# Moving the first stage's weight loads to GpSimd's queue, and packing the round trip of the inverse, in a hybrid HGRN2 and RWKV-7 layer

## The chip, the core and the metric

The kernel runs on one NeuronCore of a Trainium2 chip. The metric is device time in microseconds (us) of one execution, less being better. The kernel before takes 2757.54 us, the median of three runs (2757.54 to 2757.74).

## What is computed

One decoder layer over 2048 tokens of width 1024, in float32. Two token mixers work side by side on the columns of one input projection, then follows a ConvFFN.

```python
h = _rmsnorm(x, norm1_w[l])
proj = h @ w_in[l]                                   # 1024 -> 3840 columns
o_hg = _hgrn2_mixer(...)                             # 4 heads of 128, gated linear recurrence, chunks of 64
rw_p = rw_p + (_token_shift(rw_p) - rw_p) * rw_shift_mu[l]
o_rw = _rwkv7_mixer(...)                             # 8 heads of 64, S_t = S diag(w) + (S a) b^T + v k^T
x = x + jnp.concatenate([o_hg, o_rw], axis=-1) @ w_out[l]
x = x + _conv_ffn(_rmsnorm(x, norm2_w[l]), w_up[l], conv_w[l], conv_b[l], w_down[l])
return _rmsnorm(x, final_norm_w)
```

The kernel computes the RWKV-7 recurrence chunk by chunk. In each chunk of 64 tokens a unit triangular matrix must be inverted; its two 32x32 diagonal blocks are inverted by elimination, and the rest by small products.

## The kernel before

**Two stages.** The first stage (`phase1`, up to about 1385 us of the span) does the input projection, both mixers and the output projection of three of the four token blocks of 512. The second stage does the ConvFFN. The diff touches the first stage alone.

**The dense stream.** Products with the big weights are made in float32r from a high and a low part of each operand, three matmuls each (`mm3`, L259 to L261, into `pj`). The projection has 30 columns of 128 for each of 4 token blocks. In the first block each half column is loaded from `w_in` (256 KB, `wraw`, L550), split into `wh` and `wl` by ScalarE (L243) and VectorE (L244), and both parts are stored to a DRAM tile `Win` from GpSimd's queue (L553). In the other three blocks `wh` and `wl` are loaded back from `Win` (L557). `out_block` loads `w_out` in 32 pieces of 256 KB (`woraw`, L382) for each of three token blocks and splits them in the same way. `wh` and `wl` have 4 buffers each. `wraw` is a ring of 4 buffers that `woraw`, `oraw`, `xh` and other tiles share. All loads of weights, of tokens and of intermediate results are issued from SyncE's queue (SP), in order.

**The RWKV stream** (`rw_super`) runs 8 times, each for two pairs of heads and 512 tokens. `u` is the pair, `e` the chunk within a pair of chunks, `b` the pair of chunks, `h` the head of the pair. Its steps, by the line of their matmuls:
- L705 with L708: the products that fill `M`.
- L721: 8 DMAs copy the 32x32 diagonal blocks of `M` to DRAM (`Ed`), matrix by matrix. L723 loads them back as `E`, one matrix on each of 64 partitions.
- L729 to L755: transposes and products that need no inverse.
- L774 and L776: VectorE inverts the 64 blocks in 31 steps, into `Ti`.
- L780 and L782: `Ti` and its transpose go to DRAM (`Td`). L789 and L792 bring them back by 12 DMAs, 8 into `TTs` and 4 into `TZ`.
- L800 (`z`), L813 (`z2`) and L826 (`qus`): products with the inverse.
- ScalarE copies `qus` (PSUM) into `M` and `UV`: for `u` = 0 the part for `M` and then two for `UV`; for `u` = 1 the copies for `M` and `UV` alternate.
- L851 (`yg`), L867 and L874 (`xp`, `yp`), and L885 with L887, a chain over 8 chunks in which each product waits for VectorE's `XH` of the chunk before.

PSUM tiles of this stream come from `bank2()`, with two buffers in all, so a new tile waits until every reader of the tile before the last is done.

**The HGRN stream** (`hg_unit`) runs 16 times, with products at L965 to L1033; its VectorE steps share that engine's order with the inverse.

**Order.** The three streams are Python generators, drawn in turn; a framework's scheduler then lays the instructions out on each engine by its own costs, and each engine runs them in that order. The last token block's results (`oT`, L918 and L1039) are stored from GpSimd's queue, those of the others from SP's.

## Time and profile before

| | |
|---|---|
| Median of three runs | 2757.54 us |
| Profiled execution | 2750.25 us |
| Its span, first to last instruction | 2748.5 us |
| Mean granted clock of TensorE | 0.982 |
| TensorE matmul (PE) busy | 2645.1 us (96%) |
| VectorE (DVE) busy | 1964.0 us (71%) |
| ScalarE (ACT) busy | 1329.2 us (48%) |
| GpSimd (POOL) busy | 75.7 us (3%) |
| SP's DMA queue (q1) | 476.49 MB, 53.9% of 16 engines' span |
| GpSimd's DMA queue (q0) | 34.11 MB, 3.4% |

The profile comes from one execution, so a sum of its parts is compared with 2750.25 us, and a difference is then taken from the median of 2757.54 us. Busy matmuls are pipelined and their ends are modelled, so 96% doesn't say that TensorE runs at its peak; what matters is where it stands idle, for what it waits there, and at which clock it runs.

### The profile page before, as it was taken

What the parts mean: (1) busy time and instruction counts of PE and PEld (TensorE: products, weight loads), DVE (VectorE), ACT (ScalarE), POOL (GpSimd) and SP (SyncE); (2) the same over time, 40 slices, a digit from 0 to 9 for tenths busy, and PEclk for the clock granted to TensorE, in tenths of its full rate; (3) what the DMA queues carried; (4) which work ended last, traced back from release to release, by engine and by line L of the source; (5) the groups of instructions that cost most, each with busy time, mean ns of one, the idle gap of its engine ahead of it and who ended that gap; (6) DMA issues with size and microseconds to landing.
All of it is one profiled execution on the core that took longest, in us unless ns stands there. A gap on an engine that the chain in (4) does not pass through costs nothing.

```text
span 2748.5 us, 47939 instructions
## 1 busy us (share of the span) xinstructions
PE 2645.1 (96%) x18059; PEld 2108.0 (77%) x18059; DVE 1964.0 (71%) x3697; ACT 1329.2 (48%) x2124; POOL 75.7 (3%) x144
## 2 busy tenths in 40 slices
PE   8999999989999899999989999998999999999998
PEld 6777777767777667778668788886888888777887
DVE  5868666585576765757567789988997787667656
ACT  5455342544534444343346754555545455445544
POOL 3211000000000000000000000000000000000000
PEclk9999999989999999999999999999999999999999
DMA  9555544345653456743584467746662224999865
GB/s 302 197 163 169 166 133 127 118 133 183 209 168 120 140 158 216 239 167 121 152 279 145 126 206 260 243 143 225 220 221 75 91 86 157 312 329 311 287 195 184
DMA packets 396029, 513.68 MB, mean 187 GB/s; under 512 B 73503, under 2 KB 200853, under 8 KB 395797
## 3 DMA queue, kind: packets, MB, share of 16 engines
q1 hardware_dynamic: 385137, 476.49, 53.9%
q0 software_dynamic: 10592, 34.11, 3.4%
q8 instruction: 142, 2.33, 0.4%
q14 instruction: 90, 0.74, 0.1%
q10 hardware_dynamic: 68, 0.02, 0.0%
HBM read 373.12 MB, written 137.36 MB: 186 GB/s over the span
## 4 chain that ended last, share of the span: by engine, by line
PE 60%; DVE 7%; DMA 5%; ACT 2%; issue 2%; SPq 1%; DVEq 0%; ACTq 0%
PE ua L261 5%; PE ua L259 5%; PE ua L260 5%; PE pj L259 5%; PE pj L260 4%; PE pj L261 4%; PE ud L259 3%; PE ud L260 3%; PE ud L261 3%; PE da L260 2%; PE da L261 2%; PE da L259 2%; PE db L260 2%; PE db L259 2%; PE db L261 2%
## 5 line engine op out<-in xcount | busy, mean ns | idle before, releaser
L259 PE MATMUL pj<-hh,wh 128*128 128x512 f32 x960 | 401.8, 419 | 0.8 <-DVE xh L398 0.6
L261 PE MATMUL pj<-hh,wl 128*128 128x512 f32 x960 | 379.7, 396 | 0.4 <-DMA wl<-Win191l 0.4
L260 PE MATMUL pj<-hl,wh 128*128 128x512 f32 x960 | 379.7, 396 | 0.0
L259 PE MATMUL ua<-Bh,uwh 128*128 128x512 f32 x704 | 278.7, 396 | 14.9 <-ACT uwh L243 14.1
L261 PE MATMUL ua<-Bh,uwl 128*128 128x512 f32 x704 | 276.3, 393 | 0.3 <-DVE uwl L244 0.3
L260 PE MATMUL ua<-Bl,uwh 128*128 128x512 f32 x704 | 276.1, 392 | 0.0
L259 PEld LDWEIGHTS pj<-hh,wh 128*128 128x128 f32 x960 | 181.3, 189 | 53.4 <-issue 12.4
L260 PEld LDWEIGHTS pj<-hl,wh 128*128 128x128 f32 x960 | 181.4, 189 | 40.3 <-issue 6.0
L261 PEld LDWEIGHTS pj<-hh,wl 128*128 128x128 f32 x960 | 180.9, 188 | 39.6 <-issue 0.7
L243 ACT CAST uwh<-uraw 128x512 fp32r<-128x512 f32 x220 | 134.5, 618 | 140.9 <-PE ua L260 71.4
L243 ACT CAST dah<-draw 128x512 fp32r<-128x512 f32 x151 | 93.8, 621 | 184.6 <-PE da L260 50.5
L244 DVE TENSOR_TENSOR uwl<-uraw,uwh 128x512 fp32r<-128x512 f32 x220 | 147.3, 688 | 46.9 <-ACT uwh L243 46.8
L244 DVE TENSOR_TENSOR dal<-draw,dah 128x512 fp32r<-128x512 f32 x151 | 104.3, 690 | 104.9 <-ACT dah L243 104.6
L259 PEld LDWEIGHTS ua<-Bh,uwh 128*128 128x128 f32 x704 | 133.4, 190 | 43.7 <-ACT uwh L243 14.7
L261 PEld LDWEIGHTS ua<-Bh,uwl 128*128 128x128 f32 x704 | 133.3, 189 | 30.1 <-DVE uwl L244 2.2
L260 PEld LDWEIGHTS ua<-Bl,uwh 128*128 128x128 f32 x704 | 133.7, 190 | 27.2
L259 PE MATMUL ud<-Bh,uwh 128*128 128x512 f32 x352 | 137.8, 392 | 1.9 <-DVE cv L1357 1.9
L261 PE MATMUL ud<-Bh,uwl 128*128 128x512 f32 x352 | 137.1, 389 | 0.0
L260 PE MATMUL ud<-Bl,uwh 128*128 128x512 f32 x352 | 137.0, 389 | 0.0
L260 PE MATMUL da<-dbl,dah 128*128 128x512 f32 x340 | 134.2, 395 | 0.7 <-DVE dbl L244 0.2
L261 PE MATMUL da<-dbh,dal 128*128 128x512 f32 x340 | 133.2, 392 | 0.0
L259 PE MATMUL da<-dbh,dah 128*128 128x512 f32 x340 | 128.3, 391 | 1.6 <-ACT dbh L243 1.5
(434 smaller groups left out, 5792.2 us busy)
## 6 DMA issues: line engine op xcount, KB each, us to landing
uraw<-in_w_up_dram SPq DMA_DIRECT2D x176, 256.0 KB, 3.2
woraw<-in_w_out_dram SPq DMA_DIRECT2D x96, 256.0 KB, 3.5
draw<-Sg SPq DMA_DIRECT2D x88, 256.0 KB, 3.5
draw<-Tw SPq DMA_DIRECT2D x88, 256.0 KB, 3.7
gd<-y SPq DMA_DIRECT2D x86, 256.0 KB, 2.9
xt<-x1d SPq DMA_DIRECT2D x32, 512.0 KB, 5.3
draw<-gd SPq DMA_DIRECT2D x63, 256.0 KB, 5.0
draw<-in_w_down_dram SPq DMA_DIRECT2D x63, 256.0 KB, 5.2
```

The costliest lines, as they stand in the source:

```text
L243: S.copy(hi, src)
L244: V.tensor_sub(lo, src, hi.bitcast(F32))
L259: TE.matmul(acc, lh, rh, start=first, stop=False, skip_group_check=skip)
L260: TE.matmul(acc, lh, rl, start=False, stop=False, skip_group_check=skip)
L261: TE.matmul(acc, ll, rh, start=False, stop=last, skip_group_check=skip)
```

## The change

Three edits, all in the first stage:
- `wload` stands for GpSimd's queue, and the loads of `wraw`, of `Win` (360 of them) and of `woraw` are issued from it instead of from SP's. The 120 stores to `Win` and the last block's `oT` stores were on that queue already.
- `M` is laid out with `e` ahead of `u`, and `Ed` and `Td` have the two pairs of a block next to each other, so that one DMA serves both pairs: 4 transfers into `Ed` instead of 8, and 6 out of `Td` instead of 12. With the load of `E` and the two stores to `Td` that makes 13 for each of the 8 runs instead of 23. The bytes are the same.
- After `qus`, ScalarE makes the three copies into `M` first, for both pairs, and then the four into `UV`.

```diff
+        wload = nc.gpsimd.dma_start
...
-                        dma(raw, w_out[0, k * P:(k + 1) * P, dh * 512:dh * 512 + 512])
+                        wload(raw, w_out[0, k * P:(k + 1) * P, dh * 512:dh * 512 + 512])
...
-                            dma(raw, w_in[0, k2 * 512:k2 * 512 + 512, cols[i]:cols[i] + P].rearrange("(k p) c -> p k c", p=P))
+                            wload(raw, w_in[0, k2 * 512:k2 * 512 + 512, cols[i]:cols[i] + P].rearrange("(k p) c -> p k c", p=P))
...
-                                dma(ws[k2][c].bitcast(F32), Win[ct][k2][c])
+                                wload(ws[k2][c].bitcast(F32), Win[ct][k2][c])
...
-            for u in U:
-                for e in range(2):
-                    for q in range(2):
-                        r0 = er0(e) + 32 * q
-                        m0 = u * 32 + (e * 2 + q) * 8
-                        dma(Ed[m0:m0 + 8].rearrange("m s t -> s m t"),
-                            M[r0:r0 + 32, u, e, :, :, 32 * q:32 * q + 32].rearrange("p b h t -> p (b h) t"))
+            for e in range(2):
+                for q in range(2):
+                    r0 = er0(e) + 32 * q
+                    m0 = (e * 2 + q) * 16
+                    dma(Ed[m0:m0 + 16].rearrange("m s t -> s m t"),
+                        M[r0:r0 + 32, e, :, :, :, 32 * q:32 * q + 32].rearrange("p u b h t -> p (u b h) t"))
...
-            for u in U:
-                for e in range(2):
-                    r0 = er0(e)
-                    for q in range(2):
-                        m0 = u * 32 + (e * 2 + q) * 8
-                        dma(TTs[r0 + 32 * q:r0 + 32 * q + 32, 8 * u:8 * u + 8, 32 * q:32 * q + 32],
-                            Td[1, m0:m0 + 8].rearrange("m s t -> s m t"))
-                    m0 = u * 32 + e * 16
-                    dma(TZ[r0:r0 + 32, 0, u].rearrange("p b h t -> p (b h) t"),
-                        Td[0, m0:m0 + 8].rearrange("m s t -> s m t"))
+            for e in range(2):
+                r0 = er0(e)
+                dma(TZ[r0:r0 + 32, 0].rearrange("p u b h t -> p (u b h) t"),
+                    Td[0, 32 * e:32 * e + 16].rearrange("m s t -> s m t"))
+                for q in range(2):
+                    m0 = (e * 2 + q) * 16
+                    dma(TTs[r0 + 32 * q:r0 + 32 * q + 32, :, 32 * q:32 * q + 32],
+                        Td[1, m0:m0 + 16].rearrange("m s t -> s m t"))
...
-            for u in U:
-                quv = qus[u].rearrange("p j (b h t) -> p (j b) h t", h=2, t=P)
-                bs = slice(4 * u, 4 * u + 4)
-                if u == 0:
-                    act(M[:, u, 0, :, :, 0:64], quv[:, :, :, 0:64], AF.Copy)
+            quv = [qus[u].rearrange("p j (b h t) -> p (j b) h t", h=2, t=P) for u in U]
+            act(M[:, 0, 0, :, :, 0:64], quv[0][:, :, :, 0:64], AF.Copy)
+            for e in range(2):
+                r0, c0 = er0(e), col0(1, e)
+                act(M[r0:r0 + 64, 0, 1, :, :, 0:64], quv[1][c0:c0 + 64, :, :, 0:64], AF.Copy)
+            for u in U:
                 for e in range(2):
                     r0, c0 = er0(e), col0(u, e)
-                    if u == 1:
-                        act(M[r0:r0 + 64, u, 0, :, :, 0:64], quv[c0:c0 + 64, :, :, 0:64], AF.Copy)
-                    act(UV[r0:r0 + 64, bs, e, :].rearrange("p b (h t) -> p b h t", t=64),
-                        quv[c0:c0 + 64, :, :, 64:128], AF.Copy)
+                    act(UV[r0:r0 + 64, 4 * u:4 * u + 4, e, :].rearrange("p b (h t) -> p b h t", t=64),
+                        quv[u][c0:c0 + 64, :, :, 64:128], AF.Copy)
```

The remaining lines of the diff only follow the new order of `M`'s indices. Because the scheduler lays the program out anew, the order on the engines changes with it, up to the end of the first stage; behind it the order is the same.

More of the change, by code (lines that the diff above doesn't have):

```diff
@@ L707, in rw_super @@
                     for h in range(2):
-                        V.tensor_mul(M[:, u, :, 2 * j:2 * j + 2, h, :].rearrange("p e b t -> p b e t"),
+                        V.tensor_mul(M[:, :, u, 2 * j:2 * j + 2, h, :].rearrange("p e b t -> p b e t"),
                                      s1[:, h].rearrange("p (b e t) -> p b e t", e=2, t=P),
@@ L754, in rw_super @@
                 kr, c0, sl = 64 - er0(e), col0(u, e), (b * 2 + h) * 64
-                TE.matmul(lv[c0:c0 + 64, u, sl:sl + 64], M[kr:kr + 64, u, e, b, h, 0:64],
+                TE.matmul(lv[c0:c0 + 64, u, sl:sl + 64], M[kr:kr + 64, e, u, b, h, 0:64],
                           UV[kr:kr + 64, 4 * u + b, e, h * 64:h * 64 + 64], start=True, stop=True,
@@ L799, in rw_super @@
                 c0, sl = r0 + 32 - 32 * u, u * 256 + (b * 2 + h) * 32
-                TE.matmul(z[c0:c0 + 32, 0, sl:sl + 32], M[r0:r0 + 32, u, e, b, h, 32:64],
+                TE.matmul(z[c0:c0 + 32, 0, sl:sl + 32], M[r0:r0 + 32, e, u, b, h, 32:64],
                           TZ[r0:r0 + 32, 0, u, b, h, :], start=True, stop=True, tile_position=(r0, c0))
@@ L827, in rw_super @@
                           RHS[r0:r0 + 64, 4 * u + b, h, :], start=True, stop=True, tile_position=(r0, c0))
+            quv = [qus[u].rearrange("p j (b h t) -> p (j b) h t", h=2, t=P) for u in U]
[3 more added lines that the diff above has]
+                act(M[r0:r0 + 64, 0, 1, :, :, 0:64], quv[1][c0:c0 + 64, :, :, 0:64], AF.Copy)
             for u in U:
-                quv = qus[u].rearrange("p j (b h t) -> p (j b) h t", h=2, t=P)
-                bs = slice(4 * u, 4 * u + 4)
-                if u == 0:
-                    act(M[:, u, 0, :, :, 0:64], quv[:, :, :, 0:64], AF.Copy)
                 for e in range(2):
                     r0, c0 = er0(e), col0(u, e)
-                    if u == 1:
-                        act(M[r0:r0 + 64, u, 0, :, :, 0:64], quv[c0:c0 + 64, :, :, 0:64], AF.Copy)
-                    act(UV[r0:r0 + 64, bs, e, :].rearrange("p b (h t) -> p b h t", t=64),
-                        quv[c0:c0 + 64, :, :, 64:128], AF.Copy)
+                    act(UV[r0:r0 + 64, 4 * u:4 * u + 4, e, :].rearrange("p b (h t) -> p b h t", t=64),
+                        quv[u][c0:c0 + 64, :, :, 64:128], AF.Copy)
             yield
             for u in U:
-                Q, G = M[:, u, 0, :, :, 0:64], M[:, u, 1, :, :, 0:64]
+                Q, G = M[:, 0, u, :, :, 0:64], M[:, 1, u, :, :, 0:64]
                 yg = bank2()
@@ L848, in rw_super @@
                             for h in range(2):
-                                rhs = (M[rs_, u, e, b, h, 64:128] if w == 0
+                                rhs = (M[rs_, e, u, b, h, 64:128] if w == 0
                                        else KBT[rs_, u, 2 * b + e, h * 64:h * 64 + 64])
@@ L874, in rw_super @@
                         TE.matmul(yp[h * 64:h * 64 + 64, u, ch * 64:ch * 64 + 64],
-                                  UV[:, 4 * u + b, e, h * 64:h * 64 + 64], M[:, u, e, b, h, 64:128], start=ch == 0,
+                                  UV[:, 4 * u + b, e, h * 64:h * 64 + 64], M[:, e, u, b, h, 64:128], start=ch == 0,
                                   stop=False, tile_position=(0, h * 64), skip_group_check=True)
@@ L884, in rw_super @@
                         hr = slice(h * 64, h * 64 + 64)
-                        TE.matmul(xp[hr, u, cs_], M[hr, u, 1, b, e, 0:64], XH[hr, u, ch, :], start=False,
+                        TE.matmul(xp[hr, u, cs_], M[hr, 1, u, b, e, 0:64], XH[hr, u, ch, :], start=False,
                                   stop=ch == 7, tile_position=(h * 64, h * 64), skip_group_check=True)
```

## The prediction

> **What bounds the kernel now.** I read the windows of 200 us first, because the diff ends with the first stage. Columns: span, busy time of PE, PEld, DVE, ACT and POOL, granted clock, DMA share, GB/s.

> ```profile
> span 2748.5 us, 47939 instructions
> ```

> ```profile
> 0.00:200.00 200.00, 183.34 (x1615) 144.30 (x1616) 135.28 (x321) 100.03 (x171) 56.95 (x110) 1.00 0.69 225
> 200.00:400.00 200.00, 196.41 (x1738) 151.84 (x1738) 137.99 (x304) 97.40 (x145) 14.03 (x26) 0.98 0.48 155
> 400.00:600.00 200.00, 187.12 (x1882) 145.13 (x1880) 141.05 (x363) 76.62 (x125) 0.00 (x0) 0.99 0.43 127
> 600.00:800.00 200.00, 193.27 (x1587) 151.11 (x1588) 116.91 (x257) 95.43 (x157) 0.00 (x0) 0.97 0.60 189
> 800.00:1000.00 200.00, 188.14 (x2167) 143.78 (x2166) 129.85 (x309) 79.53 (x128) 0.00 (x0) 0.97 0.44 133
> 1000.00:1200.00 200.00, 193.93 (x1645) 150.88 (x1643) 123.98 (x277) 85.58 (x133) 0.54 (x1) 0.97 0.66 216
> 1200.00:1400.00 200.00, 185.51 (x1671) 142.21 (x1668) 128.27 (x287) 86.21 (x136) 3.07 (x5) 0.95 0.47 148
> ```

> TensorE is the bound. In these 1400 us it idles for 72 us (200 minus PE in each row, added up), and the clock takes as much as (0+0.02+0.01+0.03+0.03+0.03+0.05) x 200 = 34 us more. That is all the first stage can give. DMA is at 43% to 69%, so bytes don't bind. The built order of the changed kernel has the same instructions on PE, and the same order in the second stage. So the question is which PE waits go. Those of the first stage (us in total, times, longest):

> ```profile
> PE vps L151 <- DMA rows<-in_hg_lb_logits_dram: 9.5, 1, 9.5
> PE rw L800 <- DMA TZ<-Td: 7.6, 5, 3.4
> PE hg L1007 <- DVE hk L1000: 6.6, 5, 2.8
> PE pj L259 <- ACT wh L243: 5.7, 5, 1.8
> PE rw L851 <- ACT UV L117: 5.7, 7, 1.0
> PE hg L965 <- DVE hX L944: 4.8, 7, 1.2
> PE pj L260 <- DVE wl L244: 3.1, 4, 1.9
> ```

> The reader should see that no weight from `Win` is in it, and that the round trip's own wait is 7.6 us. What lies under the others comes from the waits of VectorE and ScalarE:

> ```profile
> DVE etmp L774 <- DMA E<-Ed: 42.1, 8, 8.5
> ACT wh L243 <- DMA woraw<-in_w_out_dram: 45.9, 24, 6.8
> ```

> **Part 1, the way back from DRAM (`Td`): -7 us.** The first of the eight round trips on SP's queue (start, length):

> ```profile
> 91.68 4.64 SPq L721 DMA_DIRECT2D Ed<-M  x8
> ...
> 143.94 1.49 SPq L792 DMA_DIRECT2D TZ<-Td  x2
> 146.72 3.09 SPq L789 DMA_DIRECT2D TTs<-Td  x6
> ...
> 150.35 0.94 SPq L789 DMA_DIRECT2D TTs<-Td  x2
> 151.34 0.45 SPq L792 DMA_DIRECT2D TZ<-Td  x1
> ```

> The last `TZ` part is the twelfth transfer and leaves at 151.8. In the changed order both `TZ` transfers come first: 143.94 + 1.49 = 145.4, so 6.4 us sooner. A transfer of twice the size lands later by between 0 and 1.7 us (2.2 us for 32 KB, 3.9 for 256 KB, rows below). The longest wait is 3.4 us, so nearly all 7.6 us go. The built order also puts 94 more dense matmuls, over the eight runs, between L755 and `z`. What is late next is ScalarE's copy behind `z`; there the order now has mostly 7 to 10 dense matmuls instead of 0 to 3. Bounds -7.6 and 0.

> **Part 2, the way out (`Ed`): -5 us.** Eight issues took 4.64 us; four take 2.3. VectorE waits for `E` 42.1 us in eight times and stops everything behind it, `hX` and `hk` too; 8 x 2.3 = 18.6 us of that go. PE waits 6.6 + 4.8 = 11.4 us for those two in the rows above; in proportion (18.6/42.1) that is 5. Bounds -11.4 and 0.

> **Part 3, the copies into `M` first: -5 us, and not for the reason that the edit suggests.** The end of `qus` in the first run:

> ```profile
> 169.27 1.20 ACT L117 ACTIVATE UV<-rw 64x512 f32<-64x512 f32 x2
> ...
> 170.84 0.69 PE L851 MATMUL rw<-M 64*64 64x64 f32 x32
> ...
> 172.07 0.58 ACT L117 ACTIVATE UV<-rw 64x512 f32<-64x512 f32 x1
> ...
> 172.70 0.69 PE L851 MATMUL rw<-M 64*64 64x64 f32 x32 [0.70 <-ACT UV L117]
> ```

> The two groups of `yg` take the PSUM buffers of the two `qus`, and these are free after the last copy out of each. Before, that is the third and the seventh copy; the second group waits 0.70 us for the seventh. Now the fifth and the seventh: the first group comes 1.2 us later (two copies of 0.6), the second no sooner. The wait between the groups closes, if PE has other work ahead of the first group. It has: in five of eight runs the built order has 31 or 32 instructions there, where mostly 8 or 9 stood. Of 5.7 us I take 5; without that cover the 0.7 us only move ahead of the group (0), or become 1.2 (8 x 0.5 = +4).

> **Part 4, the loads on GpSimd's queue: 0 us, and the widest bounds.** Rows (us to landing; mean ns of one issue; the answer for L553, the stores to `Win`):

> ```profile
> woraw<-in_w_out_dram SPq DMA_DIRECT2D x96, 256.0 KB, 3.5
> ...
> oT<-osq SPq DMA_DIRECT2D x12, 256.0 KB, 3.8
> ...
> E<-Ed SPq DMA_DIRECT2D x8, 256.0 KB, 3.9
> ...
> TZ<-Td SPq DMA_DIRECT2D x32, 32.0 KB, 2.2
> oT<-osq POOLq DMA_DIRECT2D x4, 256.0 KB, 2.4
> ```

> ```profile
> L1039 POOL DMA_DIRECT2D oT<-osq x4 | 2.2, 545 | 1045.7 <-DVE osq L1038 966.5 <-DVE etmp L774 75.0 <-DVE lastc L302 4.2
> L918 POOL DMA_DIRECT2D oT<-yo x2 | 1.4, 716 | 67.1 <-issue 67.1
> ```

> ```profile
> DMA to landing us min/median/max: 2.3/3.9/8.0
> ```

> 516 loads of 0.545 us are 281 us of 1385 on an engine that does nothing else, so the queue is no bound. The loads from `w_in` have 512 runs: 128 runs cost 545 ns and 256 cost 716, so 545 + 3 x 171 = 1058 ns each, 31 us more. `Win` loads are hidden: four buffers, and no PE wait above names them. In the first block a load stands behind the stores of the piece four before it, whose split frees its own buffer, so it waits for little that it wouldn't wait for anyway. The oT stores of the last block stand between loads too; the one with most behind it has 23 `woraw` loads behind it, but its `osq` comes early in `out_block`. The exposed ones are `woraw`: ScalarE waits for 24 of them, PE for the splits 5.7 + 3.1 = 8.8 us. A 256 KB transfer from GpSimd's queue lands after 2.4 (`oT`) to 3.9 us (`Win`), from SP's after 3.5: -1.1 to +0.4 us each. They also no longer stand behind `x1d` stores and `xh` loads. I take 0, as 3.5 is inside; bounds -8.8 and, with 24 x 0.4, +10.

> [...] Beside a copy-like VectorE step over 0.75 us, one GpSimd issue took 0.65 us instead of 0.54:

> ```profile
> 14.95 0.75 DVE L149 TENSOR_SCALAR xt<-xt,nst 128x1024 f32<-128x1024 f32 x1
> ...
> 15.17 0.65 POOL L553 DMA_DIRECT2D Win281h<-wh  x1
> ```

> [...]

> **Part 5, the clock: -7 us.** Around one of the `TZ` waits (window 940 to 965; the wait row is of 940 to 975):

> ```profile
> PE rw L800 <- DMA TZ<-Td: 5.3, 3, 3.4
> ```

> ```profile
> 940.00:965.00 25.00, 17.88 (x252) 11.74 (x253) 13.73 (x30) 11.80 (x24) 0.00 (x0) 0.73 0.60 156
> ```

> (1 - 0.73) x 25 = 6.8 us of clock are lost right where PE idled for 7 of 25 us. With the 5.3 us of waiting gone I count this one stretch as gone, and of the other 27 us none; bounds 0 and -20. [...]

> **Part 6, what it adds: +6 us.** GpSimd now issues a `w_in` load ahead of the seven small loads that PE's first instruction waits for (9.5 us): +1.1, and with the busier DMA +1.5 (bounds -1 and +4). And in the chain of L885 the built order leaves three dense matmuls or fewer at 35 of 56 steps, at 17 before. The 18 more steps have less cover if VectorE is in another instruction; one like this takes 687 ns:

> ```profile
> L244 DVE TENSOR_TENSOR wl<-woraw,wh 128x512 fp32r<-128x512 f32 x96 | 65.5, 687 | 48.3 <-ACT wh L243 47.9
> ```

> I take a third of it: 18 x 0.25 = +4.5 (bounds 0 and 12.4).

> **Sum.** -7 - 5 - 5 + 0 - 7 + 6 = -18. The profiled execution of 2750.25 us (span 2748.5) would become 2732; the median is 2757.54, so I say 2739.5.

> **Rivals.**
> - *Hidden anyway.* PE waits only change place: part 1 goes, parts 2, 3 and 5 don't. -7 + 6 = -1, so 2756.5. For it: PE has a fixed order, and an engine that is sooner does not help where its user stands late. Against: the order was laid out anew too.
> - *`woraw` becomes the bound, slower.* Place: `out_block`, 24 loads that ScalarE already waits for. Price: 0.4 us later landing plus one VectorE step of 0.75 us ahead of it = 1.15 x 24 = 28 us, on top of the forecast: 2767. It turns the sign from 18/24 = 0.75 us a load. For it: the ring is short. Against: the four `oT` stores land in 2.4 us. [...]
> - *The idle places and the clock go together.* Waits 7.6 + 11.4 + 5.7 and 20 us of clock, less 1.5: 43, so 2714.
> - *It doesn't do what it says*: part 3's edit, as told there; it is in the sum.

> **How the numbers follow.** Forecast 0.60 (own range 2725 to 2750), hidden 0.16, `woraw` 0.16, large 0.08. What can be told from no change is 0.2%, or 5.5 us. Faster 0.60 + 0.08 = 0.68, same 0.16, slower 0.16. The range of 2718 to 2766 takes in the forecast and the hidden case, reaches almost to the third with its smaller prices, and leaves out the large one.

> **What would show it.** PE's waits for `TZ` and between the `yg` groups under 1 us each in all; VectorE's for `E` near 24; clock near 1 around each `z`. Wrong: ScalarE's wait for `woraw` above 60 us; PE waits at L885 (`XH`) of more than 12 us; a landing of GpSimd's loads beyond 4.5 us.

## The result, and the profile after

The changed kernel takes 2783.93 us (median of four runs, 2776.89 to 2787.01) beside 2757.64 us for the kernel before in the same session: a ratio of 1.009, 95% interval 1.0074 to 1.0106. By the ratio it is 25 us slower where 18 us faster were forecast, and outside the range. The profiled execution took 2787.01 us, its span is 2785.2 us.

First the two stages by windows (columns as in the prediction: span, busy PE, PEld, DVE, ACT, POOL, clock, DMA share, GB/s), cut at the first matmul of the second stage. The kernel before:

```profile
0.00:1390.40 1390.40, 1318.14 (x12257) 1021.58 (x12257) 907.02 (x2104) 615.42 (x983) 74.59 (x142) 0.98 0.53 169
1390.40:2748.50 1358.10, 1326.96 (x5802) 1086.45 (x5802) 1056.96 (x1594) 713.78 (x1141) 1.09 (x2) 0.99 0.62 205
```

The kernel after:

```profile
0.00:1424.10 1424.10, 1325.81 (x12258) 1024.62 (x12258) 904.84 (x2104) 616.18 (x984) 370.20 (x658) 0.97 0.52 165
1424.10:2785.20 1361.10, 1326.88 (x5802) 1084.99 (x5802) 1055.90 (x1594) 713.86 (x1141) 1.11 (x2) 0.99 0.62 205
```

Of the 36.7 us between the two spans, 33.7 lie in the first stage: 26.0 are PE standing idle (72.3 us before, 98.3 after: window less PE) and 7.7 are PE being busy for longer. These are the clock: PE is busy for 66.6 us at half clock instead of 51.7, and when the time at half clock is counted half, its busy time in the stage is the same, 1292.3 us before and 1292.5 after. GpSimd's 370 us of issues bind nothing, as forecast; the harm lies elsewhere. PE's waits in the first stage after:

```profile
PE pj L259 <- ACT wh L243: 15.4, 16, 2.6
PE rw L798 <- DMA TZ<-Td: 13.5, 6, 4.8
PE vps L151 <- DMA cst<-in_consts_dram: 11.1, 1, 11.1
PE rw L864 <- DVE AR L854: 10.5, 6, 2.3
...
PE rw L864 <- DVE rkv L302: 3.8, 2, 2.3
PE hg L1004 <- DVE hk L997: 3.2, 4, 2.3
...
PE rw L848 <- ACT UV L117: 0.4, 2, 0.2
PE rw L882 <- DVE XH L884: 0.2, 1, 0.2
```

L798, L848, L864, L882 and L1004 are L800, L851, L867, L885 and L1007 of before. The wait for `UV` went as forecast (5.7 to 0.4), but the one at the next step, `AR` and `rkv` ahead of L864, rose from 4.4 to 14.3. The wait for `wh` rose from 5.7 to 15.4. And the wait for `TZ`, which the change was made to remove, rose from 7.6 to 13.5. ScalarE and VectorE after:

```profile
ACT wh L243 <- DMA woraw<-in_w_out_dram: 70.4, 35, 4.7
```

```profile
DVE etmp L774 <- DMA E<-Ed: 7.4, 2, 3.9
```

VectorE's wait for `E` fell from 42.1 to 7.4 us, far more than forecast, and yet no time came from it.

Why `TZ` is later is seen in the transfers issued around one round trip (10 us from just ahead of the store of `Ti`, fifth run; count, KB each, us to landing). Before:

```profile
Td<-Ti SPq DMA_DIRECT2D x1, 256.0 KB
Td<-TiT SPq DMA_DIRECT2D x1, 256.0 KB
wh<-Win191h SPq DMA_DIRECT2D x1, 256.0 KB
TTs<-Td SPq DMA_DIRECT2D x7, 32.0 KB, 1.9
TZ<-Td SPq DMA_DIRECT2D x3, 32.0 KB, 2.2
```

After:

```profile
wh<-Win191h POOLq DMA_DIRECT2D x1, 256.0 KB, 4.1
Td<-Ti SPq DMA_DIRECT2D x1, 256.0 KB
wl<-Win191l POOLq DMA_DIRECT2D x1, 256.0 KB, 5.8
Td<-TiT SPq DMA_DIRECT2D x1, 256.0 KB
wh<-Win220h POOLq DMA_DIRECT2D x1, 256.0 KB, 5.2
wl<-Win220l POOLq DMA_DIRECT2D x1, 256.0 KB, 5.7
TTs<-Td SPq DMA_DIRECT2D x4, 64.0 KB, 4.6
wh<-Win221h POOLq DMA_DIRECT2D x1, 256.0 KB, 5.5
wl<-Win221l POOLq DMA_DIRECT2D x1, 256.0 KB, 6.0
TZ<-Td SPq DMA_DIRECT2D x2, 64.0 KB
```

On SP's queue one `Win` load stood in line with the round trip, and the others waited behind it. On a queue of their own six are under way beside it, and both sides land late (a load from `Win` landed after 2.8 us in the kernel before, the median of the 93 whose landing its trace tells). Over the eight runs, 6 loads of weights were issued between the store of `Ti` and `z` in the kernel before, and 33 in the changed one. From the store of `Ti` to the first matmul of `z` it takes 10.2 us in the mean of the eight runs, where it took 7.3. That is the case for the loads as the cause; the experiments test it.

### The profile page after: what moved, and what is told of

Read it like the earlier page. It is cut to its first block, busy times and chain, and to the rows that moved or that the text cites. A ratio compares the mean times of both kernels' runs of the same rounds, so it can differ in the third digit from the quotient of the medians.

```text
span 2785.2 us, 47876 instructions
## 1 busy us (share of the span) xinstructions
PE 2652.7 (95%) x18059; PEld 2109.6 (76%) x18059; DVE 1960.7 (70%) x3697; ACT 1330.0 (48%) x2124; POOL 371.3 (13%) x660
## 4 chain that ended last, share of the span: by engine, by line
PE 44%; DMA 9%; DVE 6%; issue 3%; ACT 2%; SPq 1%; POOL 0%; DVEq 0%; ACTq 0%; POOLq 0%
PE ua L261 5%; PE ua L259 5%; PE ua L260 5%; PE ud L260 2%; PE ud L259 2%; PE ud L261 2%; PE da L260 2%; PE da L261 2%; PE da L259 2%; DMA woraw<-in_w_out_dram 2%; PE pj L259 2%; PE pj L260 2%; PE pj L261 2%; PE db L260 1%; PE db L261 1%
## 5 line engine op out<-in xcount | busy, mean ns | idle before, releaser
L259 PE MATMUL pj<-hh,wh 128*128 128x512 f32 x960 | 403.9, 421 | 2.8 <-ACT rkv L117 1.3
L260 PE MATMUL pj<-hl,wh 128*128 128x512 f32 x960 | 382.8, 399 | 0.0
L259 PE MATMUL ua<-Bh,uwh 128*128 128x512 f32 x704 | 278.8, 396 | 16.4 <-ACT uwh L243 14.3
L260 PE MATMUL ua<-Bl,uwh 128*128 128x512 f32 x704 | 276.0, 392 | 0.0
L259 PEld LDWEIGHTS pj<-hh,wh 128*128 128x128 f32 x960 | 183.0, 191 | 56.8 <-issue 14.0
L260 PEld LDWEIGHTS pj<-hl,wh 128*128 128x128 f32 x960 | 183.1, 191 | 41.0 <-issue 6.2
L243 ACT CAST uwh<-uraw 128x512 fp32r<-128x512 f32 x220 | 134.6, 617 | 139.7 <-PE ua L260 70.2
L243 ACT CAST dah<-draw 128x512 fp32r<-128x512 f32 x151 | 93.8, 621 | 185.9 <-PE da L260 53.6
L244 DVE TENSOR_TENSOR uwl<-uraw,uwh 128x512 fp32r<-128x512 f32 x220 | 146.7, 684 | 48.6 <-ACT uwh L243 48.6
L244 DVE TENSOR_TENSOR dal<-draw,dah 128x512 fp32r<-128x512 f32 x151 | 104.1, 689 | 107.6 <-ACT dah L243 107.3
L259 PEld LDWEIGHTS ua<-Bh,uwh 128*128 128x128 f32 x704 | 133.5, 190 | 45.8 <-ACT uwh L243 14.9
L260 PEld LDWEIGHTS ua<-Bl,uwh 128*128 128x128 f32 x704 | 133.7, 190 | 27.2
L259 PE MATMUL ud<-Bh,uwh 128*128 128x512 f32 x352 | 137.9, 392 | 1.6 <-DVE cv L1354 1.6
L260 PE MATMUL ud<-Bl,uwh 128*128 128x512 f32 x352 | 137.0, 389 | 0.0
L260 PE MATMUL da<-dbl,dah 128*128 128x512 f32 x340 | 133.2, 392 | 0.9 <-DVE dbl L244 0.5
L259 PE MATMUL da<-dbh,dah 128*128 128x512 f32 x340 | 128.1, 391 | 1.9 <-ACT dbh L243 1.8
## 6 DMA issues: line engine op xcount, KB each, us to landing
uraw<-in_w_up_dram SPq DMA_DIRECT2D x176, 256.0 KB, 3.2
woraw<-in_w_out_dram POOLq DMA_DIRECT2D x96, 256.0 KB, 3.5
draw<-Sg SPq DMA_DIRECT2D x88, 256.0 KB, 3.1
draw<-Tw SPq DMA_DIRECT2D x88, 256.0 KB, 3.7
gd<-y SPq DMA_DIRECT2D x86, 256.0 KB, 3.0
draw<-gd SPq DMA_DIRECT2D x63, 256.0 KB, 4.8
draw<-in_w_down_dram SPq DMA_DIRECT2D x63, 256.0 KB, 5.6
```

Of the source, the lines that this page charges most:

```text
L243: S.copy(hi, src)
L244: V.tensor_sub(lo, src, hi.bitcast(F32))
L259: TE.matmul(acc, lh, rh, start=first, stop=False, skip_group_check=skip)
L260: TE.matmul(acc, lh, rl, start=False, stop=False, skip_group_check=skip)
```

## The experiments

### One edit at a time

The three edits can be made one by one: `wload = dma` in the changed kernel (packing and copies stay), and the kernel before with the loads alone, the packing alone and the copies alone.

```diff
 # e1: the changed kernel
-        wload = nc.gpsimd.dma_start
+        wload = dma
 # e2: the kernel before, plus only
+        wload = nc.gpsimd.dma_start      # woraw, wraw and the loads from Win
 # e3: the kernel before, plus only the layout of M, 4 transfers into Ed and 6 out of Td
 # e4: the kernel before, plus only the three copies into M ahead of the four into UV
```

> The changed kernel with all its loads back on SP's queue; packing and copies stay. Theory A (the packing and the copies cost it: a 64 KB part of Td lands later than two of 32 KB did, so the way from the store of Ti to z stays near 10.2 us instead of 7.3, and the wait for UV stays turned into one for AR): only ScalarE's wait for woraw falls from 70 to some 46 us, and PE's wait for wh from 15.4 to some 6; the time falls by 5 to 12 us, to some 2774. Theory B (the loads on GpSimd's queue cost it, by their own lateness and by what they take from the round trip's transfers): the way from Ti to z falls to 7.5 us, PE's wait for TZ below 8, and the time falls to the kernel before's, 2750 to 2758.

> The kernel before with only its loads moved to GpSimd's queue. Theory A: the way from Ti to z stays near 7.3 us and PE's wait for TZ near 7.6; ScalarE's wait for woraw rises to some 70 us, and the time by 5 to 12 us, to some 2765. Theory B: the way from Ti to z rises to some 10 us, and the time to 2778 to 2785.

> The kernel before with only the new layout of M and the 4 and 6 transfers. Theory A: the way from Ti to z is some 10 us, PE's wait for TZ 10 us or more; time some 8 us above the kernel before, 2765. Theory B: way from Ti to z 7 us or less, wait for TZ below 4, time 2745 to 2757.

> The kernel before with only ScalarE's copies into M ahead of those into UV. Theory A: the wait between the yg groups (5.7 us) goes below 1, and PE's wait for AR ahead of xp rises from 3.2 by 5 to 10; time 2757 to 2763. Theory B, in which the wait for AR too comes from VectorE running late behind the loads: the 5.7 us go, AR stays near 3, time 2750 to 2754.

| | median, us | ratio to before | interval |
|---|---|---|---|
| e1 packing and copies | 2768.12 | 1.0057 | 1.0041 to 1.0073 |
| e2 loads | 2774.20 | 1.0076 | 1.0062 to 1.0089 |
| e3 packing | 2765.29 | 1.0048 | 1.0033 to 1.0063 |
| e4 copies | 2753.91 | 1.0006 | 0.9996 to 1.0017 |
| before | 2751.65 | | |

Both theories were half right. Loads and packing each cost time by themselves; the copies cost nothing and bring nothing. The three add up to 1.30%, and together they cost 0.90%. In e2 the round trip is the old one, on SP's queue, and PE still waits longer for it:

```profile
PE rw L801 <- DMA TZ<-Td: 18.8, 7, 5.0
PE pj L259 <- ACT wh L243: 12.0, 10, 2.1
```

`Ti` to `z` is 9.9 us there, as theory B had it, though the time is below the 2778 us that it named. In e1 and e3 it is 8.6 us, between the two theories. In e3 the wait for `TZ` did go, and that for `E` too, as the prediction had said; its first stage is nonetheless 13.4 us longer:

```profile
PE rw L798 <- DMA TZ<-Td: 1.8, 1, 1.8
```

```profile
DVE etmp L774 <- DMA E<-Ed: 9.2, 3, 3.2
```

```profile
0.00:1403.80 1403.80, 1328.59 (x12258) 1032.46 (x12258) 905.21 (x2104) 615.42 (x983) 75.21 (x142) 0.97 0.52 167
```

Idle is 75.2 us (72.3 before), busy 10.5 more. So the packing's cost is not waiting but clock: summed over the trace's clock records that begin in the first stage, (1 - granted clock) times the record's length is 47.8 us, and 35.8 in the kernel before. PE is busy for 79.1 us at half clock there, 51.7 before; with these counted half, its busy time is 1289.0 us, no longer than the 1292.3 before. e4 shows the exchange that the copies make:

```profile
PE rw L866 <- DVE AR L856: 6.3, 6, 1.8
PE rw L850 <- ACT UV L117: 0.6, 3, 0.2
```

5.1 us less between the `yg` groups, 3.1 more at the next step, and the time the same.

### Which loads

```diff
 # e5: the kernel before, with wload for wraw and Win only
 # e6: the kernel before, with wload for woraw only
```

> The kernel before with only the loads of w_in and Win on GpSimd's queue, woraw on SP's. Theory C (collision: on SP's queue a Win load stood in order with the round trip, two or three of them between the store of Ti and z; on a queue of their own six to eight run beside it): the way from Ti to z stays near 9.5 us, PE's wait for TZ at 12 or more, and the time rises by 12 to 18 us, to some 2766. Theory D (GpSimd's queue is late for each woraw load): ScalarE's wait for woraw stays near 46 us, the way from Ti to z near 7.5 us, time within 4 us of the kernel before.

> The kernel before with only the woraw loads on GpSimd's queue. Theory C: the way from Ti to z stays near 7.5 us, ScalarE's wait for woraw rises by 96 x some 0.3 us in its waiting third, to 52 to 56, time 3 to 8 us above the kernel before. Theory D: 15 to 22 us above it.

e5: 2776.57 us, ratio 1.0076 (1.0057 to 1.0095). e6: 2762.57 us, ratio 1.0024 (1.0012 to 1.0035). The `Win` loads, which the prediction had called hidden, cost all that the loads cost together, and PE never waits for them. It waits for what they slow. e5:

```profile
PE rw L801 <- DMA TZ<-Td: 15.9, 7, 5.0
```

Theory C holds for this wait and, in direction, for the time (21 us by the ratio, where it had 12 to 18), but `Ti` to `z` is 8.4 us, less than the 9.5 expected. In e6 `Ti` to `z` is 8.2 us, more than the 7.5 expected, but the wait for `TZ` is 6.3 us, no longer than before, and PE's wait for `wh` doubles:

```profile
PE pj L259 <- ACT wh L243: 11.6, 10, 2.1
```

Each `woraw` load is issued 0.30 us after its buffer is free, where SP took 0.03 (medians), and the issue is 0.54 us long instead of 0.33. Yet ScalarE's wait for `woraw` was not 52 us or more, but 40.9.

### More cover between z and qus

Theory E was that the packing's clock was lost because the scheduler moved dense matmuls out of the stretch from `z` to `qus`, so that PE had less to do there. Each `yield` lets the other streams put in work.

```diff
-            yield
+            for _ in range(3):
+                yield
             z2 = bank2()
 ...
-            yield
+            for _ in range(3):
+                yield
             qus = [bank2() for _ in U]
```

> The packing alone with two more yields of the RWKV stream ahead of z2 and two ahead of qus: the built order then has 169 dense matmuls between the start of z and the end of qus over the eight runs, where the packing alone had 89 and the kernel before some 153. Transfers and instructions are the same. Theory E (the packing's 13 us are clock, lost because the scheduler moved dense matmuls out of z to qus): clock lost in the first stage falls from 48 us to 36 or less, and the time to 2745 to 2756. Rival F (the loss lies in the transfers themselves, or the half clock falls where it will): the time stays at 2760 to 2770.

> The kernel before with the same four yields, as the control: 244 dense matmuls between z and qus instead of some 153. Theory E: clock lost in the first stage falls from 36 us to 28 or less; time 2740 to 2752. Rival F: the time stays within 4 us of the kernel before, or rises because the chain of the RWKV stream ends later.

e7: 2787.39 us, ratio 1.0108 (1.0092 to 1.0124). e8: 2782.57 us, ratio 1.0093 (1.0077 to 1.0108). Theory E falls, and the rival's 2760 to 2770 us for e7 was too low as well. By the traces there are 165 dense matmuls in that stretch in the kernel before, 97 in e3, 175 in e7 and 250 in e8. In e7 the clock sum fell from 47.8 to 35.8 us as expected, and the time rose all the same, from 0.48% to 1.08% above the kernel before:

```profile
0.00:1423.10 1423.10, 1337.95 (x12258) 1021.88 (x12258) 899.92 (x2101) 625.55 (x992) 74.24 (x141) 0.97 0.53 166
```

Idle is 85.2 us and busy 1338. The sum of lost clock is no price, because it counts half clock on an idle PE too. With the same sum, PE was busy for 64.9 us at half clock in e7 (54 dense matmuls began there) and for 51.7 in the kernel before (24). With these counted half, its busy time is 1305.5 us, so 13 of the 19.8 us by which it is longer are not the clock's; where they come from is left open. And e8 shows that four `yield`s alone, with no transfer, load or copy changed, cost as much as the whole change. So the order had to be held still.

### The order of the engines held

For the next runs a list of the order that the scheduler had laid out for one kernel was put into another, as order-only dependencies between neighbours on each of TensorE, VectorE and ScalarE; the built orders are then equal, instruction by instruction (e12 alone differs, by the copies after `qus`). SP's queue is not held; in e11, the loads left out, 1362 of its 1377 issues stand in the old sequence.

```diff
+    for engine, order in want.items():
+        for p, q in zip(order, order[1:]):
+            tc.add_manual_dep(by[engine][q], by[engine][p].name, no_sync, reason="order")
```

> The packing alone, with every instruction of TensorE, VectorE and ScalarE held in the order of the kernel before (by order-only dependencies between neighbours; transfers and arithmetic are those of the packing). Theory G (the packing's 13 us come from the order that the scheduler lays out around it, not from the transfers): PE's wait for TZ falls from 7.6 to some 3 us, VectorE's for E from 42 to some 25, clock lost stays near 36 us, and the time is 0 to 10 us below the kernel before. Rival H (the transfers cost it, since each of twice the size lands later): PE's wait for TZ stays at 7 us or rises, time 5 to 15 us above the kernel before.

> The kernel before, transfers and layout as they were, with the order of TensorE, VectorE and ScalarE held to that of the packing alone. Theory G: 8 to 20 us above the kernel before. Rival H: within 4 us of it.

> The kernel before with its loads on GpSimd's queue, and the order of the three engines held to that of the kernel before. If the loads' cost is their queue and the collision with the round trip: PE's wait for TZ 14 us or more, time 14 to 25 us above the kernel before. If it too came from the order: TZ 10 or less, time within 6 us of it.

> The changed kernel, all three edits, with the order of the three engines held to that of the kernel before. Theory G with the loads' own cost: the sum of the two runs above, 8 to 20 us above the kernel before. If packing makes the round trip safe from the loads: within 5 us of it.

| | median, us | ratio to before | interval |
|---|---|---|---|
| e9 packing, order of before | 2757.59 | 1.0013 | 0.9999 to 1.0027 |
| e10 transfers of before, order of e3 | 2793.53 | 1.0147 | 1.0127 to 1.0166 |
| e11 loads, order of before | 2787.13 | 1.0113 | 1.0095 to 1.0131 |
| e12 all three edits, order of before | 2797.27 | 1.0154 | 1.0134 to 1.0174 |
| before | 2753.24 | | |

The holding itself costs nothing that can be told, as far as the runs show it: the kernel before was not run with its own order held, but e9 here and e14 and e15 below have that order and lie within 0.2% of it.

**Packing.** At the old order it costs nothing that can be told; with the order laid out for it, 0.48%. Theory G is right that the order is what costs, and wrong that the transfers then gain. In e9:

```profile
0.00:1392.60 1392.60, 1319.57 (x12258) 1021.75 (x12258) 906.70 (x2104) 615.35 (x983) 74.72 (x142) 0.98 0.53 169
```

```profile
PE rw L798 <- DMA TZ<-Td: 4.7, 3, 2.1
```

```profile
DVE etmp L774 <- DMA E<-Ed: 45.1, 8, 8.4
```

The wait for `E` is not shorter at all. Where it was shorter, it was by the order: e10, with the eight transfers of before and the order of e3, has

```profile
DVE etmp L774 <- DMA E<-Ed: 3.1, 1, 3.1
```

Why four transfers don't shorten it is seen in the first way out: VectorE's last product into `M` in the kernel before, and then that product and SP's issues in e9 (start, length):

```profile
92.83 1.29 DVE L708 TENSOR_TENSOR M<-rw,cst 128x512 f32<-128x512 f32 x2 [1.18 <-PE rw L705]
```

```profile
93.22 1.29 DVE L709 TENSOR_TENSOR M<-rw,cst 128x512 f32<-128x512 f32 x2 [1.19 <-PE rw L706]
```

```profile
94.54 2.40 SPq L721 DMA_DIRECT2D Ed<-M  x4
```

Before, the first four of the eight transfers, those of the first pair, left from 91.68 on, ahead of the last product's end at 94.1. A transfer that serves both pairs must wait for the last product. Over the eight runs the last `Ed` issue ends 2.1 us after that product before, and 2.4 us after it in e9. Eight issues beside work were exchanged for four on the path. The way back is alike: in e9 the last `TZ` issue ends 3.1 us after the first began instead of 6.6 (mean of eight), but `Ti` to `z` stays at 7.3 us, since `z` could begin with the parts of its first pair.

In e10 the order of the packing without its transfers has the worst of both: it is laid out for parts that arrive sooner, and PE waits 15.7 us for `TZ`. It is 40 us slower than the kernel before, where theory G had 20 at most.

**Loads.** At the old order they cost more, not less (1.13% beside 0.76%), and the whole change too (1.54% beside 0.90%): the new order gave a part back. Both are above the ranges expected (14 to 25 and 8 to 20 us; by the ratio they are 31 and 42). Beside the loads the packing and the copies together aren't free at the old order: e12 is 0.41% above e11, and VectorE waits 58.3 us for `E` there, 47.8 in e11. e11 has the old order, the old transfers and the old queue for the round trip, so what it shows comes from the loads alone:

```profile
0.00:1428.70 1428.70, 1335.07 (x12258) 1030.16 (x12258) 906.72 (x2104) 614.37 (x983) 367.16 (x658) 0.97 0.52 164
```

```profile
PE rw L801 <- DMA TZ<-Td: 21.9, 9, 4.0
```

```profile
TTs<-Td SPq DMA_DIRECT2D x64, 32.0 KB, 3.3
TZ<-Td SPq DMA_DIRECT2D x32, 32.0 KB, 3.2
```

In the kernel before (the row of `TZ` is in the prediction):

```profile
TTs<-Td SPq DMA_DIRECT2D x64, 32.0 KB, 1.9
```

A 32 KB part of `Td`, issued from SP as ever, lands after 3.2 to 3.3 us instead of 1.9 to 2.2. These medians are of few issues, since the traces tell the landing of 13 of the 96 in e11 and of 27 before; but `Ti` to `z`, which covers all eight runs, is 9.7 us instead of 7.3. Of the 38.3 us that its first stage is longer, 21.4 are idle: PE waits 14.3 us more for `TZ`, 5.1 more for `wh` and 2.0 more ahead of its first instruction. The other 16.9 are PE at a lower clock (busy for 83.6 us at half clock instead of 51.7; with these counted half, 1293.3 us). By what mechanism the parts land later while those loads are under way, no run shows.

### Collision or lateness, and the way back alone

```diff
 # e13: e11, and the 23 transfers of the round trip by wload too
 # e14: the kernel before, with only the 12 transfers out of Td packed to 6, TZ first; 8 into Ed stay
 # e15: the kernel before, with its 12 transfers out of Td in another sequence, the 4 into TZ first
 # all three: order of the three engines as in the kernel before
```

> The kernel before with the loads and the 23 transfers of the round trip all on GpSimd's queue, the order of the three engines held to that of the kernel before. Collision: in one queue again, the loads stand behind or ahead of the round trip and not beside it; Ti to z goes back from 9.7 to 8.5 us or less, PE's wait for TZ from 22 to some 12, and the time falls below that of the loads alone at this order (2787) to 2765 to 2778. Lateness of GpSimd's queue: each of the 23 issues is later by 0.3 to 0.5 us, Ti to z rises above 10 us, PE's wait for TZ to 25 or more, time 2785 to 2800.

> The kernel before with the way back alone packed, two transfers into TZ first and then four into TTs; the way out stays at 8 transfers, so that the first four leave before the last product of M. Loads on SP's queue, order of the three engines held. If what is left of part 1 holds: PE's wait for TZ 7.6 to some 4 or less, VectorE's for E stays at 42, time 0 to 8 us below the kernel before. If the packed way back is worth nothing: within 3 us of it.

> The kernel before with its 12 transfers of the way back in another sequence, the four into TZ first, then the eight into TTs; the order of the three engines held. If the sequence is what part 1 is worth: PE's wait for TZ below 3 us, time 3 to 8 us below the kernel before; z2 and qus may wait for TTs instead, which would take it back.

e13: 2818.02 us, ratio 1.0209 (1.0186 to 1.0233). For the transfers collision was right:

```profile
TTs<-Td POOLq DMA_DIRECT2D x64, 32.0 KB, 2.1
TZ<-Td POOLq DMA_DIRECT2D x32, 32.0 KB, 2.3
```

In one queue with the loads they land as fast as ever, though GpSimd issues them (the trace tells the landing of all 96), and `Ti` to `z` is back at 7.9 us. The loads issued between the store of `Ti` and `z`, over the eight runs, are 7; they were 32 in e11 and 6 in the kernel before. For the time it was wrong: the way out now stands behind loads that wait for buffers.

```profile
DVE etmp L775 <- DMA E<-Ed: 58.5, 8, 10.6
```

VectorE waits 10.7 us more for `E` than in e11 (47.8), the inverse ends later (by 2.0 us in the mean, counted from the last product into `M`), and PE waits 21.9 us for `TZ` as in e11. Its 2818 us lie above both ranges expected, and how the 0.96% by which it is slower than e11 divides between these waits is left open.

e14: 2753.59 us beside 2759.10, ratio 0.9981 (0.9966 to 0.9996). e15: 2757.57 us, ratio 0.9992 (0.9978 to 1.0005). e14 is the one version whose interval lies below the kernel before, by 0.2%, which is about what can be told from nothing; its first stage in the profile (1391.1 us, PE waits 5.4 us for `TZ`) is that of the kernel before. In e15 PE's wait for `TZ` fell to 3.3 us, near the 3 expected, but the expected 3 us or more of time didn't come.

## Why the prediction was wrong, point by point

- **Part 4, the step that failed.** "`Win` loads are hidden... no PE wait above names them" asked only who waits for a `Win` load, not whom it slows. Put at 0 (bounds -8.8 and +10), the loads measured 0.76% by themselves, 21 us, and 1.13%, 31 us, at the old order. The `Win` loads are the larger part (e5, which moves those of `w_in` with them): with them beside it, the round trip's own transfers land later (e11: 3.2 to 3.3 us instead of 1.9 to 2.2), and in one queue with them they don't (e13: 2.1 to 2.3). That this lateness is the loads' whole price isn't shown, since e13 lost time elsewhere; in e11 the wait for `TZ` is 14.3 of the 21.4 idle us. SP's queue, read as a queue in which the round trip stands behind others, was also what held the loads back behind it (6 loads between the store of `Ti` and `z` before, 33 after). The estimate of 1058 ns for the issue of a load from `w_in` was too high as well (0.77 us in the mean of 60), but bound nothing.
- **Part 1** counted the time of the issues. They did end sooner, but `z` didn't start sooner even at the old order (7.3 and 7.35 us from `Ti`). The twelfth transfer was not what `z` began with. PE's wait for `TZ` did shrink at the old order, from 7.6 to 4.7 us (e9) and to 3.3 (e15), and the time did not.
- **Part 2** halved 4.64 us of issues that lay half beside the products into `M`. e9 has the wait for `E` at 45.1 us. Where it fell, in e3 and in the changed kernel, the order had changed (e10 has 3.1 us with the old transfers), and PE's waits for `hX` (both lines) and `hk`, by which I scaled it, did not: 14.7 us before, 15.1 in e3.
- **Part 3** had the mechanism and missed the next step. The wait between the `yg` groups went (5.7 to 0.6 in e4, 0.4 after), and `AR` came in its place; -5 measured +0.06% (-0.04 to +0.17), nothing.
- **Part 5** tied the clock to the waits at `TZ`. The clock sum rose from 35.8 to 41.0 us after, and in e3 to 47.8 with those waits down to 1.8 us. No run shows the 20 us of clock that the large rival takes off: the highest mean clock of a profiled execution is 0.985 (e14), beside 0.982 before.
- **Part 6** was sized right at the start (9.5 to 11.1 us) and too high in the chain: PE's wait at L882 is 0.2 us, not 4.5.
- **The rivals.** The slower one came nearest in time (2767, 17 us short), but by the wrong loads, so that is luck: `woraw` alone measured 0.24%, some 6.6 us, not 28. Its sign showed all the same: ScalarE's wait for `woraw` is 70.4 us, above the 60 named, but it is 40.9 with `woraw` alone moved (e6) and 52.2 with all the loads (e2). No run shows the VectorE step of 0.75 us that its price puts ahead of each load. What part 4 saw once, a longer issue beside a VectorE step, is seen again: beside VectorE's copy of `Ti` one issue took 1.08 us instead of 0.54, as these rows of the changed kernel show. But only 14 of 456 loads of `woraw` and `Win` had an issue above 0.6 us, 2 of them `woraw`.

```profile
815.59 1.06 DVE L781 COPY TiT<-Ti 64x1024 f32<-64x1024 f32 x1
```

```profile
815.69 1.08 POOL L558 DMA_DIRECT2D wl<-Win191l  x1
```

- **What no part held:** that an edit can make the scheduler lay the three engines out anew, and that this alone is worth -0.6% (e12 to the changed kernel) to +1.5% (e10). The prediction read the new order and took more cover for a gain.

## What to carry to other kernels

A queue can also be a throttle: over the eight runs, 6 loads of weights were issued between the store of `Ti` and `z` when they shared SP's queue with the round trip, and 33 from a queue of their own. Before loads are moved to a queue of their own, list what they stood behind, and price the landing of those transfers with the loads beside them. Halving the number of transfers gained nothing here (e9: ratio 1.0013), because a merged transfer waits for the last of its sources and half of the issues had stood beside other work before (the last `Ed` issue ends 2.4 us after the last product into `M` in e9, 2.1 us before); ask first whether the issue is on the path. Where a scheduler lays out the order, hold the order still in one experiment, or an edit and its new order can't be told apart.
